# Hybrid RWKV7 and NSA forward pass on one core: scaled keys loaded two units ahead, small loads on GpSimd's queue, and the second pair's heads crossed

## The chip, the cores and the metric

The kernel runs on one core of a Trainium2 chip. The metric is the device time of the whole launch in microseconds (us); lower is better. A core has five instruction streams that run side by side and wait for each other through semaphores: PE (TensorE, matmuls; PEld is its loading of weights), DVE (VectorE), ACT (ScalarE), POOL (GpSimd) and SP (SyncE, which here only issues DMAs). A matmul in fp32 appears in the records as two instructions.

## The reference

Two layers over 256 tokens of width 2048. The first is an RWKV7 mixer of 32 heads of size 64, the second a sparse attention (NSA) that the change does not touch.

```python
def wkv7_scan(r, w, k, v, a, b):
    def step(S, inp):
        r_t, w_t, k_t, v_t, a_t, b_t = inp
        sa = jnp.einsum('bhvk,bhk->bhv', S, a_t)
        S = S * w_t[:, :, None, :] + sa[..., None] * b_t[:, :, None, :] + v_t[..., None] * k_t[:, :, None, :]
        return S, jnp.einsum('bhvk,bhk->bhv', S, r_t)
...
def rwkv7_mixer(u, ...):
    xx = token_shift(u) - u
    mixed = u[None] + xx[None] * mu[:, None, None, :]
    rkvz = jnp.einsum('nbtd,nde->nbte', mixed[:4], w_rkvz)
    ...                       # decay, a, kk from small projections; heads of 64
    o = wkv7_scan(rh, heads(decay), kh, vh, -kk, kk * ah)
    mean = jnp.mean(o, axis=-1, keepdims=True)
    var = jnp.mean(jnp.square(o - mean), axis=-1, keepdims=True)
    o = ((o - mean) * lax.rsqrt(var + GN_EPS)).reshape(B, T, D) * ln_g + ln_b
    bonus = jnp.sum(rh * kh * r_k, axis=-1, keepdims=True) * vh
    o = (o + bonus.reshape(B, T, D)) * jax.nn.silu(z)
    return o @ w_o, v
```

The second layer (`nsa_shared_kv`, `nsa_mixer`) reads the residual h + y, and a last `rmsnorm` gives the output.

## The kernel before

**Stages.** The launch has three stretches. Up to about 364 us it normalises the input, projects k, v and z, and turns decay, keys and the "a" vectors into *scaled keys*, which it keeps in DRAM (`spd`: for each of 16 head pairs 128 rows of 1284 numbers, 642 KB), with v and silu(z) beside them (`vd`, `zd`). From 364 to 764 us runs the recurrence. After it come the rest of the output projection, the shared keys and values and the second layer.

**The recurrence.** Each head's 256 tokens are cut into 4 chunks of 64, and inside a chunk the recurrence is written as products with 64x64 triangular matrices, whose 32x32 diagonal blocks are inverted beforehand (`stage_t`, on DVE). Two heads make a *pair* (128 partitions: head h lies on half h, `R[h]`), two pairs (x = 0, 1) make a *unit* U; there are 8 units. A unit runs 12 steps v: for chunk c = v // 3, phase p = v % 3 of `phase`:
- p = 0: the state's part of the sums, `ARS` times S (L999), then ACT copies X (L1001);
- p = 1: the inverse `Yb` times X (L1006), then ACT copies `uv` (L1008); at c = 0 also the bonus sums (L1014), the first rows by which a unit can be told in the trace;
- p = 2: the new state (L1019, DVE L1022 to L1024), the output (L1032) and the removal of the known part for the next chunk (L987).

The matmuls among these have 64 rows and 64 columns, a quarter of the 128x128 array: L999, L1006 and L1014 (and, in `prep`, G at L929 and Y at L939, and in `turn_y` L1080) take head h of either pair from half h and leave it on half h. Only the A steps' products at L962 run from each half to both.

**What lies between the steps.** After each step `fill(FILL[v])` puts so many steps of the dense r projection into PE's order: each is three matmuls of 256 columns (L586 to L588, a high and a low half of the weights and of the input). The 16 column blocks of r need 256 such steps, 48 of them ahead of unit 0, 32 in a unit. Two blocks share one PSUM bank (`rps`). When block 2U+2+x is done, `scale_r` (at v = 1 for x = 0 and v = 6 for x = 1 of unit U, for unit U+1) multiplies it with the scaled keys: DVE L916 reads the bank and `spl` and writes `spl`'s last part, DVE L917 makes `mb`, POOL L918 and L919 copy the decays and make `ARS`. The r step that follows writes the same bank again, so it waits for `mb`. `prep` turns unit U+1's scaled keys into its matrices at v = 3 to 10 (`AUX`), while `finish` (group norm, bonus, gate) and `turn_y` handle unit U-1; POOL's L1052 takes a power for the norm (`rg`). When r is complete, the fills take steps of the output projection instead (`o_part`, three pairs of matmuls of 512 columns, L568 to L571); this begins in unit 6.

**Loads.** `spl` has two buffers (units of even and odd number). Unit U+1's scaled keys are asked for at v = 0 of unit U (`load_spl`, L865), on SP, behind the eight small loads of `Yb` for unit U+1 (L880, put at v = 11 of the unit before), and the four of `uv` (L888), and between the weight loads `wraw` (L174). The small loads of `load_a` (L872, L873) and `load_y` (L880) move pieces of 16 KB. `stage_t(1)` inverts the blocks for units 4 to 7: POOL loads them (L755), DVE works on them during units 0 to 2 (L778 to L812), ACT transposes (L816), POOL stores them (L814, L818). `load_a(4)` needs them, and the line `sch.require(lambda: U // 4 in tdone)` puts whatever is left of them into the order at once, at v = 6 of unit 2.

**What sets the order.** From the start of the recurrence PE, DVE, ACT, POOL and SP each run their instructions in the order in which the code is written (`manual_schedule`). A clock in the code, `sch.t`, decides only where pieces of `stage_t(1)` and of the weight preparation (DVE's `wlo` L186, ACT's `whi` L200) are put between them.

Of the kernel before, what the change touches and what calls it, by code (L numbers as in the profile page):

```python
# [211 lines left out]
def hybrid_kernel(ctx: ExitStack, tc: tile.TileContext, a: dict, out: bass.AP):  # L212
# [413 lines left out]
    def phase_z(nb):  # L626
        ps = two()
        yield from rows_block(ps, "z", 512, last=nb == 3)
        for tt in range(2):
# [112 lines left out]
    def stage_t(b):  # L742
# [47 lines left out]
        for lv in (8, 16):  # L790
            for g in range(32 // (2 * lv)):
                o = 2 * lv * g
                hb = lv // 2
# [81 lines left out]
    def load_y(U):
        sch.require(lambda: U // 4 in tdone)
        for x in range(2):
            for h in range(2):
                for q in range(2):
                    nc.sync.dma_start(Yb[U % 2][64 * h + 32 * q:64 * h + 32 * q + 32, x, :, 32 * q:32 * q + 32],  # L880
                                      inverse(yvd[U // 4], ((2 * U + x) % 8) * 2 + h, q))
# [40 lines left out]
    def prep(step, U):  # L922
        if step == "G":
            GY[U] = accp("sa")
            gp = GY[U][:, 0:256].rearrange("p (x c t) -> p x c t", x=2, c=NCH)
            for x in range(2):
                for c in range(NCH):
                    for h in range(2):
                        PE.matmul(gp[R[h], x, c, :], A10[R[h], x, c, :], Yb[U % 2][R[h], x, c, 32:64], start=True, **mm)  # L929
# [3 lines left out]
            sch.t += 500  # L933
        elif step == "Y":
            yp = GY[U][:, 256:512].rearrange("p (x c t) -> p x c t", x=2, c=NCH)
            for x in range(2):
                for c in range(NCH):
                    for h in range(2):
                        PE.matmul(yp[R[h], x, c, :], T00[R[h], x, c, :], GS[U][R[h], x, c, :], start=True, **mm)  # L939
# [740 lines left out]
```

## Time and profile before

| quantity | value |
|---|---|
| time of three runs: median (lowest to highest) | 1327.75 us (1323.08 to 1332.2) |
| the profiled execution's own time | 1326.59 us |
| its span (first to last instruction) | 1324.8 us |
| granted TensorE clock, mean over the span | 0.94 |
| up to the recurrence | 0 to 363.8 us |
| recurrence | 363.8 to 764.0 us, PE busy 287.0 us, clock 0.82 |
| rest | 764.0 to 1324.8 us, PE busy 550.7 us, clock 1.00 |

The times of a unit are counted from one unit's first L1014 to the next one's. In a row of the timeline stand the start and the duration in us, the engine (SPq is SP's queue, where the time of a row is the issuing), the line, the operation, what it writes and reads, its shape and its count, and in brackets the idle time before it with the instruction that ended it. The rows of the stretches give the length, the busy time of PE, PEld, DVE, ACT and POOL with instruction counts, the granted clock, the busy share of the DMA engines and GB/s.

### The profile page before, as it was taken

To read this page: it belongs to the slowest core of one execution; us is meant where nothing else is said; L and a number is where in the kernel's file an instruction comes from. 1 tells how busy PE (TensorE), PEld (TensorE's weight loads), DVE (VectorE), ACT (ScalarE), POOL (GpSimd) and SP (SyncE) were. 2 spreads that over 40 slices of the span, in tenths; PEclk is the share of its full clock that TensorE was granted. 3 is DMA by queue.
4 is the path that set the end of the run, shared out by engine and by line. 5 is a ranking of instruction groups with operands and counts; after the bars stand their busy time and mean duration, and the time that the engine had idled before them with its cause. 6 is when DMAs were issued, how large, how long until landed. Compare 5 with 4: busy or idle time off the path is not lost.

```text
span 1324.8 us, 25503 instructions
## 1 busy us (share of the span) xinstructions
PE 1184.5 (89%) x9424; PEld 1029.0 (78%) x9424; DVE 867.9 (66%) x1896; ACT 713.5 (54%) x1673; POOL 270.3 (20%) x301
## 2 busy tenths in 40 slices
PE   7999999899938756568678899999999999999997
PEld 6788998878837656557666688888889999999887
DVE  6999776798934467234334568767547688776555
ACT  4667776666613323223334457666556666666553
POOL 2300154244330110111010000101023333333101
PEclk9999999998969787688679999999999999999999
DMA  6558877758776432544332467587665635463763
GB/s 218 166 182 247 223 237 235 198 178 237 218 157 147 125 105 68 170 113 104 94 113 93 148 209 245 176 265 222 207 172 151 160 99 141 120 158 114 272 205 112
DMA packets 243517, 225.26 MB, mean 170 GB/s; under 512 B 64016, under 2 KB 191424, under 8 KB 243008
## 3 DMA queue, kind: packets, MB, share of 16 engines
q1 hardware_dynamic: 242528, 220.98, 56.6%
q0 software_dynamic: 864, 2.65, 0.8%
q8 instruction: 74, 1.21, 0.4%
q14 instruction: 51, 0.42, 0.1%
HBM read 200.48 MB, written 23.10 MB: 169 GB/s over the span
## 4 chain that ended last, share of the span: by engine, by line
PE 76%; DVE 9%; DMA 6%; issue 3%; ACT 2%; SPq 2%; POOL 2%; DVEq 0%; ACTq 0%; POOLq 0%
PE bank L569 13%; PE bank L571 13%; PE bank L568 13%; PE bank L586 7%; PE bank L588 6%; PE bank L587 6%; PE bank L228 4%; DVE wlo L186 2%; DMA spl<-spd 2%; PE pair L999 1%; PE pair L1032 1%; SPq L888 1%; DMA wraw<-in_a_w_rkvz_dram 1%; DMA invA<-abd 1%; POOL sp L716 1%
## 5 line engine op out<-in xcount | busy, mean ns | idle before, releaser
L186 DVE TENSOR_TENSOR wlo<-wraw,whi 128x512 fp32r<-128x512 f32 (+2 forms) x612 | 437.3, 727 | 147.3 <-ACT whi L200 144.7
L200 ACT ACTIVATE whi<-wraw 128x512 fp32r<-128x512 f32 (+2 forms) x664 | 402.2, 619 | 219.4 <-PE bank L571 97.6
L586 PE MATMUL bank<-mh,whi 128*128 128x256 f32 (+1 forms) x800 | 247.3, 309 | 82.6 <-DVE mb L917 82.3
L569 PE MATMUL bank<-wlo,mh 128*128 128x512 f32 (+3 forms) x640 | 244.4, 383 | 4.0 <-DVE wlo L186 3.9
L571 PE MATMUL bank<-whi,ml 128*128 128x512 f32 (+3 forms) x640 | 242.0, 382 | 0.0
L588 PE MATMUL bank<-mh,wlo 128*128 128x256 f32 (+1 forms) x800 | 235.0, 294 | 0.8 <-DVE wlo L186 0.8
L587 PE MATMUL bank<-ml,whi 128*128 128x256 f32 (+1 forms) x800 | 235.0, 294 | 0.0
L586 PEld LDWEIGHTS bank<-mh,whi 128*128 128x128 f32 (+1 forms) x800 | 158.8, 199 | 92.1 <-DVE mb L917 64.0
L568 PE MATMUL bank<-whi,mh 128*128 128x512 f32 (+3 forms) x640 | 218.3, 382 | 4.0 <-ACT mh L412 2.4
L587 PEld LDWEIGHTS bank<-ml,whi 128*128 128x128 f32 (+1 forms) x800 | 159.6, 200 | 1.9
L588 PEld LDWEIGHTS bank<-mh,wlo 128*128 128x128 f32 (+1 forms) x800 | 159.0, 199 | 2.5 <-DVE wlo L186 1.0
L569 PEld LDWEIGHTS bank<-wlo,mh 128*128 128x128 f32 x640 | 121.2, 189 | 26.4 <-DVE wlo L186 7.5
L568 PEld LDWEIGHTS bank<-whi,mh 128*128 128x128 f32 x640 | 120.0, 189 | 23.9 <-ACT mh L412 2.6
L571 PEld LDWEIGHTS bank<-whi,ml 128*128 128x128 f32 x640 | 121.1, 189 | 19.6 <-issue 0.4
L186 POOL TENSOR_TENSOR wlo<-wraw,whi 128x512 fp32r<-128x512 f32 (+2 forms) x52 | 67.8, 1306 | 190.2 <-ACT whi L200 158.4
L569 PE MATMUL bank<-wlo,kvh 128*128 128x512 f32 x192 | 76.9, 401 | 0.0
L571 PE MATMUL bank<-whi,kvl 128*128 128x512 f32 x192 | 76.1, 396 | 0.0
L568 PE MATMUL bank<-whi,kvh 128*128 128x512 f32 x192 | 67.4, 396 | 0.0
L1073 ACT ACTIVATE O<-pair,nmr,rg 128x64 f32<-128x64 f32 x64 | 21.1, 401 | 66.2 <-DVE nmr L1059 66.2
L1042 DVE BATCH_NORM_STATS2 sta<-pair 128x6 f32<-128x64 f32 x64 | 13.8, 216 | 61.6 <-ACT X L1001 60.9
L1001 ACT ACTIVATE X<-pair 128x128 f32<-128x128 f32 x32 | 8.9, 277 | 81.3 <-PE pair L999 60.7
L412 ACT ACTIVATE mh<-mtmp 128x256 fp32r<-128x256 f32 x96 | 38.9, 410 | 22.3 <-DVE mtmp L419 20.7
(318 smaller groups left out, 1894.0 us busy)
## 6 DMA issues: line engine op xcount, KB each, us to landing
wraw<-in_a_w_rkvz_dram SPq DMA_DIRECT2D x128, 512.0 KB, 4.8
wraw<-in_kv_w_dram SPq DMA_DIRECT2D x48, 512.0 KB, 4.3
wraw<-in_b_w_in_dram SPq DMA_DIRECT2D x40, 512.0 KB, 4.3
wraw<-in_a_w_o_dram SPq DMA_DIRECT2D x32, 512.0 KB, 4.2
wraw<-in_b_w_o_dram SPq DMA_DIRECT2D x32, 512.0 KB, 3.6
spd<-sp SPq DMA_DIRECT2D x16, 642.0 KB, 5.0
spl<-spd SPq DMA_DIRECT2D x16, 642.0 KB, 5.3
wraw<-in_b_w_in_dram SPq DMA_DIRECT2D x24, 384.0 KB, 3.3
```

Of the source, the lines that this page charges most:

```text
L186: eng.tensor_tensor(lv, src, hv.bitcast(F32), op=OP.subtract)
L200: self.nc.scalar.activation(hv, src, AF.Copy)
L228: return fn(*args, **kw)
L412: S.activation(h, src, AF.Copy)
L568: PE.matmul(o, mh[:, ts], wh[:, 0, :], start=k == ends[0], stop=False)
L569: PE.matmul(o, mh[:, ts], wl[:, 0, :], start=False, stop=False)
L571: PE.matmul(o, ml[:, ts], wh[:, 0, :], start=False, stop=k == ends[1])
L586: PE.matmul(o, wh[:, s, :], mh, start=k == 0 and first, stop=False, **kw)
L587: PE.matmul(o, wh[:, s, :], ml, start=False, stop=False, **kw)
L588: PE.matmul(o, wl[:, s, :], mh, start=False, stop=k == NK - 1, **kw)
L1042: V.bn_stats(sta[:, x, c, :], view(U, 192 + 64 * c, 64)[:, x])
L1073: S.activation(O[:, x, i, :], view(U, 192 + 64 * i, 64)[:, x], AF.Identity, scale=rg[:, x, i:i + 1], bias=nmr[:, x, i:i + 1])
```

## The change

**Scaled keys.** At v = 0 of unit U the kernel now asks for unit U+2's scaled keys instead of unit U+1's, into the buffer that unit U has given up. The weights, scaled keys and v needed first are asked for ahead of the rest in the prologue, where `scale_r(0, 0)`, 8 r steps, the load of unit 1's scaled keys, 8 r steps and `scale_r(0, 1)` follow each other.

**Queues.** `load_a`, `load_y` and the last block of z are issued by GpSimd, the rest by SP as before. Around unit 4, SP's order before is the following; `spl_4673` and `spl_4674` are the scaled keys of unit 5's two pairs, which `scale_r` uses a step later in the same unit.

```order
L174 DMA wraw<-in_a_w_rkvz_dram 128x8x128
L880 DMA Yb_4670<-yvd_1623 32x4x32 x8
L888 DMA uv_4676<-vd 64x4x64 x4
L865 DMA spl_4673<-spd 128x1284
L865 DMA spl_4674<-spd 128x1284
L174 DMA wraw<-in_a_w_rkvz_dram 128x8x128 x2
```

Now, at the same place, the two buffers named 4670 and 4671 are those of unit 6.

```order
L176 DMA wraw<-in_a_w_rkvz_dram 128x8x128
L893 DMA uv_4675<-vd 64x4x64 x4
L868 DMA spl_4670<-spd 128x1284
L868 DMA spl_4671<-spd 128x1284
L176 DMA wraw<-in_a_w_rkvz_dram 128x8x128 x2
L903 DMA gb<-in_a_ln_g_dram 64x4x64
```

The loads of `Yb` have left SP's order there, and the scaled keys in it are used one unit later. On POOL, around v = 0 of a unit, stood:

```order
L1052 TENSOR_TENSOR rg<-rg,half 128x8
L885 MEMSET uv_4675 64x8x64 x2
L918 COPY pc<-spl_4671 128x4
L919 TENSOR_TENSOR ars_4681<-spl_4671 128x384
L918 COPY pc<-spl_4672 128x4
L919 TENSOR_TENSOR ars_4682<-spl_4672 128x384
L1052 TENSOR_TENSOR rg<-rg,half 128x8
```

Now the small loads of the next unit's blocks stand ahead of it (`a` and `t` are `A10` and `T00`):

```order
L875 DMA a_4666<-abd 32x4x32
L877 DMA t_4667<-tnd_1621 32x4x32
L885 DMA Yb_4668<-yvd_1623 32x4x32 x8
L1051 TENSOR_TENSOR rg<-rg,half 128x8
L890 MEMSET uv_4674 64x8x64 x2
L927 COPY pc<-spl_4670 128x4
L928 TENSOR_TENSOR ars_4680<-spl_4670 128x384
```

What moved: eight issues of `Yb` now come directly ahead of the power for the norm (`rg`, now L1051), which DVE's `nmr` waits for. `nmr` itself is now issued after `v` in step 1.

**Crossed heads.** For the second pair, `H(1, h)` is the other half: its operands `A10`, `T00`, `Yb`, X, O and the loads that fill them lie on half 1-h. So of the four 64x64 matmuls of a step, two run from a half to itself and two to the other half; the matmuls are written chunk by chunk with the pairs inside. G and Y now share a tile of two banks, and A0, A1 write that tile and one more bank, with DVE's three masks (M0, M1, M2) set apart; `turn_y` handles both pairs in one step.

**The inverses of the second half.** `stage_t(1)` starts 9000 ns later by the code's clock, and its costliest steps are counted at 1.8 instead of 2.4 times. On DVE, at v = 6 of unit 2, stood behind `scale_r`'s product:

```order
L917 TENSOR_TENSOR mb<-bank_4701,spl_4674 128x256
L811 TENSOR_TENSOR invX<-invT,invM 128x512
L812 TENSOR_REDUCE invT<-invX 128x8x8
L811 TENSOR_TENSOR invX<-invT,invM 128x1024
L812 TENSOR_REDUCE invT<-invX 128x8x8
L811 TENSOR_TENSOR invX<-invT,invM 128x1024
L812 TENSOR_REDUCE invT<-invX 128x8x8
L186 TENSOR_TENSOR wlo<-wraw,whi 128x512
```

and now stands:

```order
L926 TENSOR_TENSOR mb<-bank_4700,spl_4673 128x256
L803 TENSOR_TENSOR invX<-invA,invT 128x512
L804 TENSOR_REDUCE invM<-invX 128x8x8
L813 TENSOR_TENSOR invX<-invT,invM 128x512
L814 TENSOR_REDUCE invT<-invX 128x8x8
L813 TENSOR_TENSOR invX<-invT,invM 128x512
L814 TENSOR_REDUCE invT<-invX 128x8x8
L813 TENSOR_TENSOR invX<-invT,invM 128x1024
L814 TENSOR_REDUCE invT<-invX 128x8x8
L813 TENSOR_TENSOR invX<-invT,invM 128x1024
L814 TENSOR_REDUCE invT<-invX 128x8x8
L188 TENSOR_TENSOR wlo<-wraw,whi 128x512
```

The pieces of `stage_t(1)` that are put there at once have grown from three pairs of product and sum to five.

**The end.** In unit 6 all r steps are placed by v = 7 (`FILLL`) and none after; the output projection's steps start in unit 7, four r steps' worth at a time.

```diff
-AUX = {3: ("G",), 4: ("B0",), 5: ("Y",), 6: ("B1",), 7: ("A0",), 8: ("A1",), 9: ("A2", "T0"), 10: ("T1",)}
+AUX = {3: ("G",), 4: ("B0",), 5: ("Y",), 6: ("B1",), 7: ("A0",), 8: ("A1",), 9: ("M0", "M1"), 10: ("T", "M2")}
+AUXL = {3: ("G",), 4: ("B0",), 5: ("Y",), 6: ("B1",), 7: ("A0",), 9: ("A1",), 10: ("T", "M0", "M1"), 11: ("M2",)}
+FILLL = (2, 2, 2, 2, 2, 2, 2, 2, 0, 0, 0, 0)
...
-            store_heads(zd, nb, tt, th)
+            store_heads(zd, nb, tt, th, G if nb == 3 else nc.sync)
...
-        yield 500.0
+        yield 9000.0 if b else 500.0
...
-                        yield DT * (2.4 if b else 1.0)
+                        yield DT * (1.8 if b else 1.0)
...
-    psum = open_psum((("bank", 0), ("bank", 1), ("bank", 2), ("bank", 3), ("pair", 0), ("pair", 1)))
-    banks(acc=(0,), sa=(1, 2, 3))
+    psum = open_psum((("bank", 0), ("bank", 1), ("pair", 2), ("pair", 0), ("pair", 1)))
+    banks(acc=(0,), sa=(1,))
...
+    H = lambda x, h: R[h ^ x]
...
-                    nc.sync.dma_start(Yb[U % 2][64 * h + 32 * q:64 * h + 32 * q + 32, x, :, 32 * q:32 * q + 32],
-                                      inverse(yvd[U // 4], ((2 * U + x) % 8) * 2 + h, q))
+                    at = 64 * (h ^ x) + 32 * q
+                    G.dma_start(Yb[U % 2][at:at + 32, x, :, 32 * q:32 * q + 32],
+                                inverse(yvd[U // 4], ((2 * U + x) % 8) * 2 + h, q))
...
+            for c in range(NCH):
+                for x, h in each:
+                    PE.matmul(gp[R[h], x, c, :], A10[H(x, h), x, c, :], Yb[U % 2][H(x, h), x, c, 32:64], start=True, **mm)
...
-                        PE.matmul(o[R[h], x], ARS[U % 2][x][R[h], k, c - 1, :], st[R[h], x, :], start=False, **mm)
+                        PE.matmul(o[H(x, h), x], ARS[U % 2][x][R[h], k, c - 1, :], st[R[h], x, :], start=False, **mm)
...
-                PE.matmul(pu[R[h], x], Yb[U % 2][R[h], x, c, :], XS[U][R[h], x, :], start=False, **mm)
+                PE.matmul(pu[R[h], x], Yb[U % 2][H(x, h), x, c, :], XS[U][H(x, h), x, :], start=False, **mm)
...
+    W.late = True
+    load_spl(0)
     load_a(0)
-    load_spl(0)
     load_y(0)
+    fill(8)
     load_v(0)
-    W.late = True
-    fill(2)
+    load_y(1)
+    fill(8)
+    scale_r(0, 0)
     phase_done.add("scan")
-    load_y(1)
+    fill(8)
     load_spl(1)
-    load_v(1)
-    fill(14)
-    scale_r(0, 0)
-    fill(16)
+    fill(8)
     scale_r(0, 1)
...
-                    if U + 1 < NU:
-                        load_v(U + 1)
-                if 0 < U and U + 1 < NU:
-                    load_spl(U + 1)
+                if U + 1 < NU:
+                    load_v(U + 1)
+                if U + 2 < NU:
+                    load_spl(U + 2)
...
-            if v == 6 and U + 1 < NU:
+            if v == (6 if U + 2 < NU else 8) and U + 1 < NU:
                 scale_r(U + 1, 1)
...
-                for step in {1: ("nmr", "v", "02"), 2: ("25",), 3: ("58", "b"), 4: ("g",), 7: ("+",), 8: ("z",)}.get(v, ()):
+                for step in {1: ("v", "nmr", "02"), 2: ("25",), 3: ("58", "b"), 4: ("g",), 7: ("+",), 8: ("z",)}.get(v, ()):
...
-            fill(FILL[v] if "r" not in phase_done else FILLO)
+            fill(FILLO if U + 1 == NU else FILLL[v] if U + 2 == NU else FILL[v])
```

More of the change, by code (lines that the diff above doesn't have):

```diff
@@ L923, in prep @@
         if step == "G":
[L924 to L929, printed above, removed]
+            GY[U] = pair_tile(2).rearrange("p (x c) -> p x c", x=2)
+            gp = GY[U][:, :, 0:128].rearrange("p x (c t) -> p x c t", c=NCH)
+            for c in range(NCH):
+                for x, h in each:
+                    PE.matmul(gp[R[h], x, c, :], A10[H(x, h), x, c, :], Yb[U % 2][H(x, h), x, c, 32:64], start=True, **mm)
             gs = scan.tile([128, 2, NCH, 32], F32, name="gs", bufs=1)
@@ L932, in prep @@
             GS[U] = gs
-            sch.t += 500
+            sch.t += 550
         elif step == "Y":
[L935 to L939, printed above, removed]
+            yp = GY[U][:, :, 128:256].rearrange("p x (c t) -> p x c t", c=NCH)
+            for c in range(NCH):
+                for x, h in each:
+                    PE.matmul(yp[H(x, h), x, c, :], T00[R[h], x, c, :], GS[U][R[h], x, c, :], start=True, **mm)
             for h in range(2):
@@ L951, in prep @@
             sch.t += 300
+        elif step[0] == "A":
+            x = int(step[1])
+            if x == 0:
+                AT[U] = (pair_tile(2), accp("sa"))
+            both, m = AT[U]
+            BK, pp, kr, ar = parts(U, x)
+            for c in range(NCH):
+                o = x * 256 + c * 64
+                for e in range(2):
+                    for h in range(2):
+                        k = h ^ e
+                        PE.matmul(both[R[k], h * 512 + o:h * 512 + o + 64], BK[R[h], c, k, :], ar[R[h], 1, c, :], start=True, **mm)
+                for h in range(2):
+                    PE.matmul(m[R[1 - h], o:o + 64], BK[R[h], c, 1 - h, :], ar[R[h], 0, c, :], start=True, **mm)
+            sch.t += 900
@@ L1009, in phase @@
             if c == 0:
-                for x in range(2):
-                    for i in range(NCH):
-                        for h in range(2):
-                            o = x * 512 + 448 + 2 * i
-                            PE.matmul(PBK[U][R[h], o:o + 2], mb[R[h], x, 64 * i:64 * i + 64], ones2[R[h]], start=False, **mm)
+                for i in range(NCH):
+                    for x, h in each:
+                        o = x * 512 + 448 + 2 * i
+                        PE.matmul(PBK[U][H(x, h), o:o + 2], mb[R[h], x, 64 * i:64 * i + 64], ones2[R[h]], start=False, **mm)
             sch.t += 200
@@ L1188, in hybrid_kernel @@
     fill(LASTFILL - 2)
-    for x in range(2):
-        turn_y(U, x)
-        fill(3)
+    turn_y(U)
     for _ in dense:
```

102 lines of the change are left out of this document (43 added, 59 removed).

## The prediction

> **What bounds the kernel now.** The page's costliest groups came first. On one line PE stands idle for long behind DVE, which is not busy there.
>
> ```profile
> L586 PE MATMUL bank<-mh,whi 128*128 128x256 f32 (+1 forms) x800 | 247.3, 309 | 82.6 <-DVE mb L917 82.3
> ```
>
> Next the waits from 330 to 780 us (who <- releaser: sum, count, longest), to see what DVE itself waits for:
>
> ```profile
> PE bank L586 <- DVE mb L917: 82.3, 13, 20.2
> ...
> DVE spl L916 <- DMA spl<-spd: 63.7, 6, 14.7
> ```
>
> So an r step waits for `mb`, and DVE for the scaled keys. Where it lies in a unit the timeline of unit 4 shows:
>
> ```profile
> 582.94 2.32 SPq L880 DMA_DIRECT2D Yb<-yvd  x5
> 583.90 1.10 PE L1014 MATMUL pair<-ones,mb 64*64 64x2 f32 x32 [0.75 <-ACT uv L1008]
> 585.35 2.51 SPq L888 DMA_DIRECT2D uv<-vd  x4
> 587.95 1.02 SPq L865 DMA_DIRECT2D spl<-spd  x2
> 592.72 0.42 DVE L916 TENSOR_TENSOR spl<-bank,spl 128x256 f32<-128x256 f32 x1 [11.19 <-DMA spl<-spd]
> 593.53 0.58 PE L586 MATMUL bank<-mh,whi 128*128 128x256 f32 x1 [8.53 <-DVE mb L917]
> 613.33 0.39 PE L586 MATMUL bank<-mh,whi 128*128 128x256 f32 x1 [1.41 <-DVE mb L917]
> ```
>
> SP asks for the keys at 588, once the small loads are out; PE needs them at 585 and stands 8.53 us. The second `scale_r` costs 1.41: DVE's two products, whose data are there. Then the stretches, cut at the units' first L1014 (us, busy PE, PEld, DVE, ACT, POOL, clock, DMA share, GB/s); the last two rows split unit 4 after its stall:
>
> ```profile
> 394.40:408.60 14.20, 13.46 (x240) 12.38 (x239) 8.87 (x20) 5.76 (x14) 2.00 (x3) 1.00 0.81 188
> 408.60:440.40 31.80, 28.31 (x462) 24.87 (x462) 15.58 (x48) 11.11 (x30) 3.88 (x6) 0.95 0.55 137
> 440.40:482.40 42.00, 30.94 (x496) 27.36 (x496) 22.43 (x56) 14.04 (x40) 3.52 (x6) 0.84 0.33 95
> 482.40:536.80 54.40, 32.68 (x496) 28.79 (x496) 32.56 (x57) 16.27 (x44) 8.69 (x12) 0.75 0.39 120
> 536.80:583.90 47.10, 31.18 (x494) 27.59 (x494) 16.84 (x43) 14.13 (x40) 5.10 (x8) 0.78 0.42 120
> 583.90:628.90 45.00, 32.96 (x494) 29.22 (x494) 16.84 (x43) 14.13 (x40) 5.35 (x8) 0.77 0.44 113
> 628.90:673.30 44.40, 32.97 (x494) 29.22 (x494) 16.85 (x43) 14.12 (x40) 5.36 (x8) 0.77 0.35 102
> 673.30:719.60 46.30, 34.20 (x479) 27.75 (x479) 19.41 (x48) 15.18 (x42) 4.59 (x6) 0.82 0.34 105
> 719.60:764.00 44.40, 39.93 (x368) 29.94 (x369) 23.08 (x57) 21.06 (x54) 1.64 (x1) 1.00 0.42 131
> 586.10:606.40 20.30, 12.41 (x110) 11.26 (x111) 5.95 (x14) 5.67 (x17) 1.52 (x3) 0.50 0.38 112
> 606.60:630.30 23.70, 20.35 (x385) 17.76 (x383) 10.89 (x29) 8.25 (x23) 3.84 (x4) 1.00 0.49 114
> ```
>
> Unit 0 loads no keys, has no stall and takes 31.8 us; units 1 to 6 take 279.2 together. A stall is paid twice: PE idles, and the clock stands at 0.50 for the next 20 us.
>
> **Part 1: keys two units ahead.** They are now asked for a whole unit (some 30 us) before use; before, 4.8 us passed from request (587.95) to DVE's start (592.72). The first-`scale_r` stall goes from units 1 to 6, and with it the slow clock. What is late next is DVE's 1.41, twice a unit, as unit 0 shows it. A stall-free unit is therefore unit 0's 31.8, less 1.5 for its clock of 0.95, plus 1.2 for `turn_y`'s matmuls (two of the row below), which unit 0 lacks: 31.5. Unit 4 gives the same by another way: 45.0 − 8.5 − about 5 (half of what PE did in 20.3 us at half clock) = 31.5.
>
> **Part 2: crossed heads.** The timeline of unit 4 has both kinds of matmul, 64x64 in two quadrants and in four; the last row is from the chain of waits in the prologue:
>
> ```profile
> 608.80 1.12 PE L939 MATMUL bank<-gs,t 64*64 64x32 f32 x32
> 610.76 0.68 PE L999 MATMUL pair<-S,ars 64*64 64x64 f32 x16
> 618.23 0.69 PE L962 MATMUL bank<-spl 64*64 64x64 f32 x32
> 622.61 0.63 PE L1080 MATMUL pair<-cst,O 64*64 64x64 f32 x16
> ...
> 403.13 1.08 PE bank L975 x32
> ```
>
> 32 records take 0.69 in four quadrants (L962) and 1.08 to 1.12 in two (L939, L975): 0.41 less. A unit has 48 such records of L999 and 32 each of L1006, L1014, G, Y and `turn_y`, 208 in all: 208/32 × 0.41 = 2.7 us. The bounds: nothing, if some other limit holds these matmuls; 3.5 if all halve (7 us at 1.1 per 32). I take 2.7, since L962 runs the very pattern.
>
> **Part 3: issues on POOL.** Each steady unit gives POOL 16 issues. POOL's rows nearest to them are the loads of the inverses (median issue in ns in the middle), the power for the norm, and a store beside a DVE product:
>
> ```profile
> L755 POOL DMA_DIRECT2D invA<-abd x8: 628/628/732, 369.7 to 374.2; - x8
> ...
> 626.03 2.01 POOL L1052 TENSOR_TENSOR rg<-rg,half 128x8 f32<-128x8 f32 x1 [12.17 <-DVE rg L1051]
> ...
> 519.60 0.68 DVE L186 TENSOR_TENSOR wlo<-wraw,whi 128x512 fp32r<-128x512 f32 x1
> ...
> 519.98 0.65 POOL L814 DMA_DIRECT2D tnd<-invT  x1 [8.32 <-DVE invT L812]
> ```
>
> At 0.63 us, 16 issues are 10 us on top of POOL's 5.35 in unit 4, far below the unit's length. But the eight of `Yb` wait for the last reader of that buffer (L1006 at v = 10) and stand ahead of the power: 5 us, with some 3 us between that reader and the next unit's statistics, so `rg` comes about 2 us late. DVE's `nmr`, queued before `scale_r`'s next work, passes some of it on; the move of `v` ahead of `nmr` takes part of that away. I take +0.4 us a unit. SP loses 16 issues of 0.46 each (2.32 for five); its weights had the time before too: nothing. A steady unit: 31.5 − 2.7 + 0.4 = 29.2.
>
> **Part 4: unit 2.** Here DVE does the forced rest of the inverses:
>
> ```profile
> 503.31 1.09 DVE L801 TENSOR_TENSOR invX<-invA,invT 128x512 f32<-128x512 f32 x1
> ...
> 505.04 0.68 DVE L186 TENSOR_TENSOR wlo<-wraw,whi 128x512 fp32r<-128x512 f32 x1
> ...
> 510.98 1.58 DVE L811 TENSOR_TENSOR invX<-invT,invM 128x512 f32<-128x512 f32 x1
> ...
> 513.32 1.94 DVE L811 TENSOR_TENSOR invX<-invT,invM 128x1024 f32<-128x1024 f32 x1
> ...
> 522.45 0.69 PE L1019 MATMUL pair<-uv,bkt 128*64 128x64 f32 x8 [7.88 <-ACT uv L1008]
> ```
>
> Three product-and-sum pairs run from 510.98 to 519.60 (where `wlo` follows), and PE stands 7.88, since ACT's transposes of the result lie ahead of its `uv` copy. The order now has five pairs; the two new ones have 512 elements, at the 1.73 from 503.31 (a product; its sum follows) to 505.04: +3.5. So unit 2 is 29.2 + 11.4 for this stall + 3 for 3.2 us pairs (513.32 to 519.60 holds two) that stand ahead of the state's addition in the steps before + 6 for some 12 us of its rest at half clock: 49.6.
>
> The clock: unit 4's row has 0.50 for 20.3 us after a stall. The Trainium skill ("TensorE: Matmul & The Clock Gate", "Part 1: The HAM clock gate") has the full rate back after a busy window of about 3.4 us; by that the 6 would be an estimated 1.7 and the sum 1231. The trace does not agree, so the sum keeps 6.
>
> **Part 5: unit 6, the prologue and the end.** In unit 6 16 r steps go instead of 32; three matmuls of an r step take the 0.36 between the starts of their successors (613.79, then 614.15), so 29.2 − 5.8 + 1 for latency that fewer fills leave bare = 24.4. Unit 0: 31.8 − 2.3 (no `turn_y`) = 29.5.
>
> ```profile
> 613.79 0.28 PE L586 MATMUL bank<-mh,whi 128*128 128x256 f32 x1
> 614.15 0.28 PE L586 MATMUL bank<-mh,whi 128*128 128x256 f32 x1
> ...
> 382.98 0.18 DVE L761 COPY invT<-invA 128x16 f32<-128x16 f32 x1 [6.98 <-DMA invA<-abd]
> 386.03 0.55 PE L586 MATMUL bank<-mh,whi 128*128 128x256 f32 x1 [20.24 <-DVE mb L917]
> ...
> 758.70 0.39 PE L569 MATMUL bank<-wlo,mh 128*128 128x512 f32 x1
> ```
>
> The prologue's 20.24 ends at 386.03. DVE's copy for the inverses waits for POOL's loads until 382.98, and `scale_r` stands behind it; `stage_t(1)` now starts later, and the keys come first in SP's order. Then G is first to wait, for `A10` and `Yb`. On POOL, from the recurrence's start at 364: four stores of z at 0.63 (2.5), memsets (2, an estimate), 16 issues at 0.63 (10), and some 3 until the last has landed: 382. From G to the first L1014 the stretch from 394.4 took 14.2 us at full clock; less two crossed groups 13.4, plus 3.6 for a clock still low: 399, where before 408.6; I would not be surprised by 393 or 404.
>
> The output projection leaves unit 6, where the fills from v = 6 on held 5.1 of its steps (k), each six 512-column matmuls at 0.68 per three (from an L569 to the next, 758.70): 7.0 go to the end. Add 3 for unit 7, whose thinner fills may let the clock fall, less 1.2 for its crossed matmuls: +8.8.
>
> **Sum.** L1014 of unit 7 comes at 399 + 29.5 + 4 × 29.2 (units 1, 3, 4, 5) + 49.6 + 24.4 = 619.3, before 719.6: −100.3. With +8.8: −91.5. The profiled execution took 1326.6 (span 1324.8), 1.2 under the median of the three runs; 1326.6 − 91.5 = 1235.
>
> **Rivals.** *The crossing buys nothing.* L962's four quadrants write one PSUM bank for each row half, whereas every two-quadrant row above writes one bank from both halves, as the crossed matmuls of a pair still do; so the bank and not the quadrant may set the time. Then 2.7 × 7.5 = 20 us fall out: 1255. Chance 0.17. The Trainium skill ("TensorEngine Tiling (Array Packing)", "Gotcha 1: PSUM Pressure") states that different row tiles cannot use the same bank at once; by it this rival would hold. No row here separates the two.
>
> *POOL's issues cost 1.2 us* where other work runs: `rg` 4.6 us later in seven units, +32: 1267. For it: L755's longest is 0.73 in a quiet stretch; against: L814's 0.65 beside DVE's `wlo`. Chance 0.10.
>
> *More gain:* the prologue's G at 377, no clock fall in unit 7, the state's addition in unit 2 not held up, crossing at 3.5: −5 −3 −6 −6 = 1215. Chance 0.08.
>
> *POOL becomes the bound (slower).* Unit length is then 5.4 + 16 t for an issue time t. It decides from 29.2 = 5.4 + 16 t, t = 1.5; the kernel is slower than before from t = (44.4 − 5.4)/16 = 2.4. At 2.6 a unit takes 47, so 8 × 17.8 = +143: 1378. 0.65 beside a DVE product speaks against it. Chance 0.03. The Trainium skill ("SBUF — State Buffer", "A bandwidth-pool intuition that's wrong (but worth ruling out)") puts a GpSimd-issued DMA at 620 ns alone and 3100 ns beside a DVE copy, held back for its descriptors; an estimate by that is 5.4 + 16 × 3.1 = 55 a unit, some 1440. The trace agrees on the first figure and, in its one overlapped issue, not on the second.
>
> *The load ahead does not act*, because SP reaches it late behind its own waits for weight buffers: stalls stay, with the crossing and the queue as forecast: 1297. In unit 4 SP's rows follow each other without a wait from 582.94 to 588.97. Chance 0.02.
>
> **Numbers.** Forecast 1235 at 0.60. The range reaches down into the gain case and up to the POOL case: 1212 to 1268. The measurement tells about 1%, 13 us, from no change. Faster 0.93; slower 0.04 (POOL as bound, and a mishap of its size); within 1% 0.03.
>
> **What would show it.** Right: no L586 wait above 2 us on `mb` in units 1 to 6, units of about 29 at clock 1.00, 32 records of L939's successor at 0.7, POOL rows near 0.63, one long PE wait in unit 2 of 11 us. Wrong: POOL issues above 1 us with DVE's `nmr` waiting on `rg`; G, Y or L1006 at 1.1 per 32; or a stall on `spl<-spd` again.

## The result and the profile after

The changed kernel takes 1250.37 us (median of 4 runs, 1248.05 to 1252.28) against 1327.62 before: a ratio of 0.9417 (95% interval 0.9379 to 0.9456), 77 us less. The forecast was 1235 with a range of 1212 to 1268: right in sign and inside the range, 15 us too low. The profiled execution took 1252.2 (span 1250.4), 17.1 above the forecast's sum, and the stretches below show where these 17.1 lie.

From the page of the changed kernel, the engines and the group that stood 82.6 us before; from its waits, the same pair with its count and longest wait. Line numbers are the changed kernel's (L588 was L586, L926 was L917, L1013 was L1014).

```profile
PE 1162.2 (93%) x9424; PEld 1007.8 (81%) x9424; DVE 867.1 (69%) x1896; ACT 712.3 (57%) x1673; POOL 343.8 (27%) x433
...
L588 PE MATMUL bank<-mh,whi 128*128 128x256 f32 (+1 forms) x800 | 246.0, 307 | 14.5 <-DVE mb L926 14.3
...
PE bank L588 <- DVE mb L926: 14.3, 14, 2.1
```

The stalls of 6.6 to 12.0 us in units 1 to 6 have gone; what is left is DVE's own 1.4 once a unit, 0.5 once a unit and 2.1 in the prologue. No wait of DVE for the scaled keys is left among the larger ones.

The stretches from one unit's first L1013 to the next (units 0 to 6, then the rest; columns as before):

```profile
399.20:432.01 32.81, 28.57 (x463) 24.92 (x463) 17.27 (x59) 11.20 (x30) 11.20 (x20) 0.84 0.58 152
432.01:464.14 32.13, 27.80 (x495) 24.17 (x495) 21.20 (x61) 13.93 (x40) 13.88 (x24) 0.89 0.54 142
464.14:512.54 48.40, 30.74 (x495) 26.78 (x495) 36.55 (x62) 16.15 (x44) 17.20 (x26) 0.79 0.49 140
512.54:544.70 32.16, 27.83 (x495) 24.23 (x495) 16.16 (x43) 13.90 (x40) 14.30 (x24) 0.89 0.60 157
544.70:576.83 32.13, 27.80 (x494) 24.18 (x495) 16.13 (x43) 13.90 (x40) 14.14 (x24) 0.89 0.59 157
576.83:607.58 30.75, 26.42 (x491) 22.93 (x492) 16.05 (x43) 13.90 (x40) 13.76 (x24) 0.94 0.50 145
607.58:636.44 28.86, 22.57 (x449) 18.94 (x449) 15.27 (x42) 12.28 (x38) 5.58 (x8) 0.88 0.32 91
636.44:1250.40 613.96, 597.20 (x3572) 517.34 (x3572) 413.44 (x912) 363.82 (x837) 115.80 (x104) 0.99 0.57 174
```

| place | before | forecast | after | after − forecast |
|---|---|---|---|---|
| first bonus matmul of unit 0 | 408.6 | 399 | 399.2 | +0.2 |
| unit 0 | 31.8 | 29.5 | 32.8 | +3.3 |
| units 1, 3, 4, 5 | 41.9, 47.1, 45.0, 44.4 | 29.2 each | 32.1, 32.2, 32.1, 30.8 | +10.4 |
| unit 2 | 54.4 | 49.6 | 48.4 | −1.2 |
| unit 6 | 46.3 | 24.4 | 28.9 | +4.5 |
| from unit 7 to the end of the span | 605.2 | 614.0 | 614.0 | 0.0 |

So the prologue, unit 2 and the end came as forecast; units 0, 1 and 3 to 6 are longer by 1.6 to 4.5 us each, and in all of them the granted clock is 0.84 to 0.94, where the forecast had 1.00 (in unit 0 the 0.95 of before).

**Where the clock falls.** The timeline of the changed kernel around v = 1 of unit 4, PE beside ACT and DVE:

```profile
543.53 0.34 PE L1006 MATMUL pair<-X,Yb 64*64 64x64 f32 x8
544.08 0.57 ACT L1008 ACTIVATE uv<-pair 64x128 f32<-64x128 f32 x2 [0.74 <-PE pair L1006]
544.70 0.64 PE L1013 MATMUL pair<-ones,mb 64*64 64x2 f32 x32 [0.82 <-ACT uv L1008]
545.37 0.42 DVE L926 TENSOR_TENSOR mb<-bank,spl 128x256 f32<-128x256 f32 x1 [1.31 <-PE pair L1013]
545.85 0.42 PE L588 MATMUL bank<-mh,whi 128*128 128x256 f32 x1 [0.51 <-DVE mb L926]
```

From 543.87 to 545.85 PE does nothing but 0.64 us of matmuls of two columns: it waits for the copy of `uv` (its bank is read there), then DVE waits for the bonus matmuls (they read the `mb` that it is to overwrite), then PE for DVE. Cut at steps of 3.41 us, the stretches behind are:

```profile
542.69:546.10 3.41, 2.07 (x50) 1.72 (x49) 1.89 (x5) 1.19 (x5) 3.28 (x5) 1.00 0.86 210
546.10:549.52 3.42, 2.96 (x25) 2.55 (x26) 1.77 (x5) 1.69 (x5) 1.81 (x3) 0.50 0.90 250
549.52:552.93 3.41, 3.41 (x47) 3.07 (x44) 0.09 (x1) 1.51 (x5) 0.00 (x0) 0.50 0.93 323
559.76:563.17 3.41, 1.98 (x36) 1.61 (x37) 3.03 (x9) 1.28 (x3) 1.93 (x3) 1.00 0.55 115
```

The window with the hole is followed by two at clock 0.50; the full one among these is the last slow one. This hole became the first theory for the missing 17 us; the runs below test it.

### The profile page after: what moved, and what is told of

It is laid out like the page before. It is cut to its first block, busy times and chain, and to the rows that moved or that the text cites. A ratio compares the mean times of both kernels' runs of the same rounds, so it can differ in the third digit from the quotient of the medians.

```text
span 1250.4 us, 25597 instructions
## 1 busy us (share of the span) xinstructions
PE 1162.2 (93%) x9424; PEld 1007.8 (81%) x9424; DVE 867.1 (69%) x1896; ACT 712.3 (57%) x1673; POOL 343.8 (27%) x433
## 4 chain that ended last, share of the span: by engine, by line
PE 75%; DVE 11%; DMA 4%; issue 3%; ACT 3%; POOL 2%; SPq 1%; ACTq 0%; DVEq 0%; POOLq 0%
PE bank L571 12%; PE bank L573 12%; PE bank L570 12%; PE bank L588 8%; PE bank L589 6%; PE bank L590 6%; PE bank L230 4%; DVE wlo L188 3%; PE pair L573 1%; PE pair L570 1%; PE pair L1031 1%; PE pair L571 1%; ACT whi L202 1%; DMA Yb<-yvd 1%; DVE invX L803 1%
## 5 line engine op out<-in xcount | busy, mean ns | idle before, releaser
L588 PE MATMUL bank<-mh,whi 128*128 128x256 f32 (+1 forms) x800 | 246.0, 307 | 14.5 <-DVE mb L926 14.3
L571 PE MATMUL bank<-wlo,mh 128*128 128x512 f32 (+3 forms) x608 | 231.8, 382 | 5.2 <-DVE wlo L188 5.1
L573 PE MATMUL bank<-whi,ml 128*128 128x512 f32 (+3 forms) x608 | 228.4, 380 | 0.0
L570 PE MATMUL bank<-whi,mh 128*128 128x512 f32 (+3 forms) x608 | 204.7, 380 | 1.7 <-ACT mh L414 1.5
L588 PEld LDWEIGHTS bank<-mh,whi 128*128 128x128 f32 (+1 forms) x800 | 157.4, 197 | 24.1 <-DVE mb L926 14.2
L571 PEld LDWEIGHTS bank<-wlo,mh 128*128 128x128 f32 x608 | 115.3, 190 | 26.5 <-DVE wlo L188 8.7
L570 PEld LDWEIGHTS bank<-whi,mh 128*128 128x128 f32 x608 | 113.8, 189 | 20.3 <-ACT mh L414 1.7
L573 PEld LDWEIGHTS bank<-whi,ml 128*128 128x128 f32 x608 | 115.3, 190 | 17.7 <-issue 0.4
L421 DVE SCALAR_TENSOR_TENSOR mtmp<-xx,prm,xn 128x256 f32<-128x256 f32 x96 | 48.8, 517 | 0.6 <-POOL xx L506 0.5
```

The lines of the kernel that those rows point to most:

```text
L421: V.scalar_tensor_tensor(m, xx[:, k, :], mu[:, k:k + 1], xn[:, k, 1:], op0=OP.mult, op1=OP.add)
L570: PE.matmul(o, mh[:, ts], wh[:, 0, :], start=k == ends[0], stop=False)
L571: PE.matmul(o, mh[:, ts], wl[:, 0, :], start=False, stop=False)
L573: PE.matmul(o, ml[:, ts], wh[:, 0, :], start=False, stop=k == ends[1])
L588: PE.matmul(o, wh[:, s, :], mh, start=k == 0 and first, stop=False, **kw)
```

## The experiments

Every ratio is against the kernel before on the same chip, so kernels are compared by their ratios; the changed kernel stands at 0.9417.

### The bonus matmuls moved out of the hole

```diff
             if c == 0:
                 removal(U, 0)
+                for i in range(NCH):
+                    for x, h in each:
+                        o = x * 512 + 448 + 2 * i
+                        PE.matmul(PBK[U][H(x, h), o:o + 2], mb[R[h], x, 64 * i:64 * i + 64], ones2[R[h]], start=False, **mm)
...
-            if c == 0:
-                for i in range(NCH):
-                    for x, h in each:
-                        o = x * 512 + 448 + 2 * i
-                        PE.matmul(PBK[U][H(x, h), o:o + 2], mb[R[h], x, 64 * i:64 * i + 64], ones2[R[h]], start=False, **mm)
```

> The changed kernel, with the 16 bonus matmuls (L1013) issued at v = 0, right after the removal, instead of v = 1 between the uv copy and the r steps. Theory 'hole': the 17 us by which the recurrence is longer than forecast come from a hole of about 2 us at v = 1 of each unit (0.82 waiting for uv, 0.64 of two-column matmuls, 0.51 waiting for mb), after which the granted clock is 0.50 for some 7 us. Without the hole the clock of units 1, 3, 4 rises from 0.89 to 0.97 or more and a unit goes from 32.1 to 27.5 to 28.5: 25 to 30 us less, 1220 to 1226. Rival 'waits only': the clock falls for another reason; just the bare waits go, 1.3 us in 7 units: 1241, clock still 0.89.

Measured: 1239.70 us, ratio 0.9348 (0.9319 to 0.9377), some 10 us less. The total is what the rival named, but not by the rival's way. Units 3 to 6 and the 63 us after them (the marker now stands at v = 0, some 3 us earlier in each unit):

```profile
506.90:538.35 31.45, 27.03 (x498) 23.50 (x494) 16.67 (x45) 14.02 (x40) 14.57 (x26) 0.95 0.64 170
538.35:567.20 28.85, 25.29 (x498) 22.01 (x495) 16.07 (x45) 13.90 (x40) 13.47 (x24) 1.00 0.66 175
567.20:596.04 28.84, 25.27 (x498) 22.00 (x495) 16.06 (x45) 13.90 (x40) 13.44 (x24) 1.00 0.55 158
596.04:620.41 24.37, 18.85 (x451) 16.25 (x447) 14.79 (x44) 11.72 (x36) 6.09 (x9) 0.99 0.38 103
620.41:683.41 63.00, 57.93 (x442) 43.96 (x442) 32.91 (x75) 29.19 (x70) 4.42 (x4) 0.90 0.44 139
```

Units 4 and 5 take 28.85 us at clock 1.00, unit 6 24.4. Units 3 to 6 gain 10.4 us together, units 0 to 2 4.3. Some 4 are given back: at the start, where the first removal (L987) comes 2.1 later (397.37 against 395.29), and from unit 7 on, where the clock is 0.90 in the first 63 us instead of 0.97. With the hole gone the clock of units 4 and 5 is 1.00, as its theory said; the 25 to 30 us that it gave for the total were wrong, since the clock falls in other places too.

### The hole filled, with nothing moved

Three idle matmuls stand ahead of the bonus matmuls, two behind them, in units 0 to 6.

```diff
             if c == 0:
+                idle = pair_tile(2) if U + 1 < NU else None
+                for n in range(3 if U + 1 < NU else 0):
+                    PE.matmul(idle[:, 0:128], ident, ident, start=True, **mm)
                 for i in range(NCH):
...
+                for n in range(2 if U + 1 < NU else 0):
+                    PE.matmul(idle[:, 0:128], ident, ident, start=True, **mm)
```

> The changed kernel with five idle 128x128 matmuls (an identity by itself, into a PSUM tile that nobody reads) in units 0 to 6 at v = 1: three ahead of the bonus matmuls, two behind them. No wait of the program's own work is taken away; they only fill PE's hole, and can delay the r steps by some tenths. Theory 'hole': the clock no longer falls at v = 1, units 1, 3, 4 take 28.5 to 30 us instead of 32.1, about 10 us less as with the bonus matmuls moved, 1236 to 1245. Rival 'wait': the time went because the program's own waits went, not for the clock; then the fill gives nothing, or costs up to 4 us: 1250 to 1254.

Measured: 1239.55 us, ratio 0.9352 (0.9314 to 0.9390). The timeline at v = 1 of unit 3, and units 3 to 5:

```profile
504.38 0.34 PE L1006 MATMUL pair<-X,Yb 64*64 64x64 f32 x8
504.65 0.94 PE L1012 MATMUL pair<-cst 128*128 128x128 f32 x6
505.55 0.64 PE L1016 MATMUL pair<-ones,mb 64*64 64x2 f32 x32
506.12 0.71 PE L1018 MATMUL pair<-cst 128*128 128x128 f32 x4
506.71 0.39 PE L588 MATMUL bank<-mh,whi 128*128 128x256 f32 x1
...
505.55:535.31 29.76, 26.76 (x505) 23.33 (x505) 16.17 (x43) 13.93 (x40) 14.31 (x24) 1.00 0.57 154
535.31:566.47 31.16, 28.17 (x505) 24.66 (x505) 16.12 (x43) 13.94 (x40) 14.16 (x24) 0.95 0.62 161
566.47:595.85 29.38, 26.38 (x502) 22.97 (x501) 16.05 (x43) 13.93 (x40) 13.79 (x24) 1.00 0.53 151
```

Work that serves no result, put where PE stood idle, makes the kernel 9 to 11 us faster (by the ratios and by the medians; the two intervals overlap by 0.0011). Nothing of the program's own work became earlier (from the end of L1006 to the first L588 it is 1.99 us here and was 1.98); only the clock changed. That settles it against the rival: with clock 1.00 units 3 and 5 take 29.8 and 29.4 us, and 29.2 was the forecast. Unit 4 still falls to 0.95, behind its second `scale_r` (last section).

### The crossing undone, with and without the filled hole

In `load_a` and `load_y`, 64 * h stands for 64 * (h ^ x) as well. (`T00` lies on half h in either kernel; of the products that read it, Y, it is the output that crosses.)

```diff
-    H = lambda x, h: R[h ^ x]
+    H = lambda x, h: R[h]
```

> The changed kernel without the crossing: both pairs' heads lie on their own halves again, all else as changed. Theory 'quadrants' (the forecast's term of 2.7 us a unit): 32 records go from 0.64 to about 1.1, a unit grows by 2.7, the whole by about 20 us: 1270. Rival 'bank': the crossing bought nothing in time: 1250 within 5.

Measured: 1278.21 us, ratio 0.9644 (0.9601 to 0.9688), about 30 us longer than the changed kernel. More than the 20 expected; unit 6 and the end came 4.5 and 7 us longer, and the clock swings from unit to unit, as units 3 and 4 show, which run the same instructions:

```profile
519.44:551.53 32.09, 27.98 (x495) 24.63 (x495) 16.91 (x43) 13.79 (x40) 14.86 (x25) 1.00 0.57 146
551.53:587.77 36.24, 32.13 (x494) 28.44 (x494) 16.92 (x43) 13.93 (x40) 14.13 (x25) 0.86 0.54 139
```

So the same edit was held against the kernel with the filled hole:

> The changed kernel without the crossing and with the five idle matmuls at v = 1, to be held against the crossed kernel with the same idle matmuls (units of 29.2 to 31.2 us at a clock near 1.00, 1239.6 us in all). Theory 'quadrants': at equal clock a unit is 2.7 longer, 32 us; the whole 18 to 24 us longer: 1258 to 1264; the other 8 us of the 28 that the straight kernel lost were the clock. Rival: the crossing is worth 3.5 to 4 us a unit by itself: 1268 to 1272.

Measured: 1262.10 us, ratio 0.9528 (0.9500 to 0.9555), 0.0176 above the crossed one: 23 us. Units 3 to 5:

```profile
513.97:546.12 32.15, 29.19 (x506) 25.86 (x505) 16.25 (x43) 13.93 (x40) 15.17 (x25) 1.00 0.54 142
546.12:578.24 32.12, 29.17 (x506) 25.84 (x505) 16.87 (x43) 13.82 (x40) 14.12 (x24) 1.00 0.64 157
578.24:610.03 31.79, 28.83 (x503) 25.50 (x502) 16.89 (x43) 13.82 (x40) 13.80 (x23) 1.00 0.51 142
```

At equal clock the crossing is worth 2.4 us a unit (32.15 against 29.76, 31.79 against 29.38), near the forecast (2.7). What the rest of the 30 was is not told apart: the profiled executions differ by 23 us without the filled hole (spans of 1273.7 and 1250.4) and by 20 with it (1258.7 and 1238.7), and without it the clock differs in both directions (units 0, 3 and 5 at 1.00 in the straight kernel, units 1 and 4 at 0.86, unit 6 at 0.80).

### The small loads back on SP

The same is done for `T00` and `Yb`.

```diff
-                G.dma_start(A10[at:at + 32, x, :, 0:32],
+                nc.sync.dma_start(A10[at:at + 32, x, :, 0:32],
```

> The changed kernel with A10, T00 and Yb loaded on SP's queue again, all else as changed. Forecast's theory: POOL's queue costs 0.4 us a unit through the power for the norm, so 3 us less inside the units; the prologue's G, which now waits for POOL's 16 issues until 382, comes up to 5 us earlier: 1242 to 1250. Rival 'POOL queue': the missing 17 us are those of the issues on POOL (rg, nmr late): 1230 to 1235.

Measured: 1244.27 us, ratio 0.9384 (0.9362 to 0.9406): 4 us less, with an interval that overlaps the changed kernel's. The units hardly change (31.6, 47.2, 31.8, 32.1 for units 1 to 4; 2.4 us less in units 0 to 6 together); where the clock is the same there is no difference (unit 4: 32.1 in both at 0.89, unit 6: 28.8 and 28.9 at 0.88). The first bonus matmul comes at 395.0 instead of 399.2. So POOL's queue costs the prologue about 4 us, and in the units no cost is seen. On POOL in the changed kernel, the loads' issue (median in the middle, ns) and the power for the norm ahead of unit 4:

```profile
L885 POOL DMA_DIRECT2D Yb<-yvd x64: 548/548/551, 371.0 to 605.9; - x64
...
539.90 3.25 POOL L885 DMA_DIRECT2D Yb<-yvd  x6
543.17 1.79 POOL L1051 TENSOR_TENSOR rg<-rg,half 128x8 f32<-128x8 f32 x1
```

The power starts 0.35 after DVE's last statistics (542.82) and ends at 544.96, before DVE, which is held by the bonus matmuls until 545.37, could take it.

### The keys late again in the changed kernel, and early in the kernel before

```diff
-                if U + 2 < NU:
-                    load_spl(U + 2)
+                if 0 < U and U + 1 < NU:
+                    load_spl(U + 1)
```

> The changed kernel with each unit's scaled keys asked for at v = 0 of the unit before, as in the kernel before, all else as changed. Theory: the mb stalls of units 1 to 6 return, 5 to 9 us each (SP's queue is shorter by eight issues of 0.46) and 5 us of slow clock each in place of today's 3: 6 x (7 + 2) = +54, 1295 to 1320. Rival 'the queue did it': with the small loads off SP the keys arrive in time anyway: under 1265.

Measured: 1289.53 us, ratio 0.9725 (0.9699 to 0.9752): 41 us longer. The timeline around v = 1 of unit 4:

```profile
565.44 1.02 SPq L868 DMA_DIRECT2D spl<-spd  x2
569.83 0.42 DVE L925 TENSOR_TENSOR spl<-bank,spl 128x256 f32<-128x256 f32 x1 [7.83 <-DMA spl<-spd]
570.64 0.58 PE L588 MATMUL bank<-mh,whi 128*128 128x256 f32 x1 [6.73 <-DVE mb L926]
```

The stall returns, 5.6 to 7.4 us in each of units 1 to 6, although SP has no `Yb` load ahead of the keys any more. The total is 5 us below the range: the six stalls make 37 of the 41 us, so the slow clock added less than 1 us a unit where 2 were expected; the units had one anyway.

The other way round, the one edit in the kernel before:

> The kernel before with one edit: at v = 0 of unit U it asks for unit U+2's scaled keys instead of unit U+1's. Theory: the mb stalls of units 1 to 6 (53.5 us together) go and with them 2 to 5 us of slow clock each; unit 2 keeps its 7.9 for the inverses; prologue and end stay as they are: 62 to 83 us less, 1243 to 1265. Rival 'needs the queue too': with the small loads still on SP ahead of them the keys or the weights behind them come late and half of the stalls stay: 1290 or more.

Measured: 1268.69 us, ratio 0.9568 (0.9548 to 0.9587): 57 us less, 4 short of the expected range. No stall on the keys is left, but an ordinary unit takes 34.3 at clock 0.90, not the 31.5 at 1.00 that the forecast's first part had:

```profile
521.35:555.65 34.30, 30.33 (x494) 26.73 (x494) 16.48 (x43) 14.05 (x40) 5.53 (x8) 0.90 0.58 159
```

This single edit makes three quarters of the whole gain.

### The inverses of the second half spread out

```diff
-                        yield DT * (1.8 if b else 1.0)
+                        yield DT * ((0.8 if lv == 8 else 2.2) if b else 1.0)
...
-                yield DT * (0.6 if b else 0.25)
+                yield DT * (0.3 if b else 0.25)
```

> The changed kernel with the pieces of the second half's inverses spread otherwise (factors 0.3 for the small levels, 0.8 for the middle and 2.2 for the last level), so that none is left to be put at once at v = 6 of unit 2; the same work in all. Theory: unit 2's 48.4 is its 11.06 wait for the inverses, the DVE products ahead of the state's addition and the slow clock behind; the wait goes, the products stay: unit 2 at 35 to 39, the others as they were, 9 to 13 us less: 1237 to 1242. Rival 'DVE is full there': the same 20 us of products delay the state's additions by as much: 1246 to 1252.

Measured: 1245.23 us, ratio 0.9382 (0.9357 to 0.9406), between the two cases and with an interval that overlaps the changed kernel's. In the changed kernel PE waits 11.06 in unit 2 (first row); with the pieces spread, units 1 and 2 are:

```profile
498.57 0.69 PE L1018 MATMUL pair<-uv,bkt 128*64 128x64 f32 x8 [11.06 <-ACT uv L1008]
```

```profile
432.96:469.77 36.81, 29.08 (x495) 25.35 (x495) 29.49 (x63) 13.92 (x40) 13.96 (x24) 0.86 0.48 134
469.77:507.75 37.98, 31.66 (x494) 27.52 (x494) 24.01 (x50) 16.11 (x44) 16.45 (x26) 0.78 0.62 178
```

Unit 2 gains 10.4, unit 1 loses 4.7, where DVE's busy time rises from 21.2 to 29.5: nearly half of the gain is lost again, since the products now stand in DVE's order there.

### Joined kernels

The first joins the bonus matmuls at v = 0, all small loads on SP and the spread inverses.

> The changed kernel with bonus matmuls at v = 0, small loads on SP and the inverses spread, as in the three runs that did one of these each. If the effects add: 1250 - 10 - 5 - 11 = 1224 (1218 to 1232). If the slow clock only moves on to another place: 1232 to 1240.

Measured: 1233.54 us, ratio 0.9309 (0.9275 to 0.9342): the effects do not add. The profiled execution, the longest of the four (a span of 1239.6), shows a new wait in unit 3: G waits for `Yb`. The run with only the small loads on SP has no such wait above 0.4 us in its units; why it comes here stays open.

```profile
505.62 0.99 PE L937 MATMUL pair<-Yb,a 64*64 64x32 f32 x6 [3.25 <-DMA Yb<-yvd]
```

The second therefore leaves the small loads on POOL, but for unit 0's (A10, T00 and Yb), puts the bonus matmuls at v = 0 and two idle matmuls at v = 1, and lets the inverses start earlier in the prologue (the flag "scan" starts `stage_t(1)`); the lines of the bonus and idle matmuls are like those above and are left out here:

```diff
-                G.dma_start(A10[at:at + 32, x, :, 0:32],
+                (G if U else nc.sync).dma_start(A10[at:at + 32, x, :, 0:32],
...
     load_y(0)
+    phase_done.add("scan")
...
-    phase_done.add("scan")
...
-                        yield DT * (1.8 if b else 1.0)
+                        yield DT * ((0.6 if lv == 8 else 2.0) if b else 1.0)
...
-                yield DT * (0.6 if b else 0.25)
+                yield DT * (0.25 if b else 0.25)
```

> The changed kernel with bonus matmuls at v = 0, two idle matmuls at v = 1 of units 0 to 6, the small loads of unit 0 alone on SP (the rest stays on POOL), and the second half's inverses started in the prologue and spread (factors 0.25, 0.6, 2.0), none left for one burst. Theory: no hole, no late Yb (which the run with all small loads on SP had in its fourth unit), unit 2 without its 11 us: units of 29 at clock 1.00, unit 2 at 34 to 38, first L1013 at 393 to 396: 1215 to 1226. Rival 'DVE is full': the spread inverses delay units 0 to 2 by what the burst cost: 1228 to 1236.

Measured: 1220.76 us, ratio 0.9215 (0.9184 to 0.9245): 2.1% below the changed kernel (0.9215/0.9417), the fastest of all. Units 1, 2 and 4:

```profile
423.88:460.49 36.61, 30.28 (x501) 26.30 (x499) 32.11 (x61) 15.06 (x42) 13.84 (x23) 0.81 0.49 137
460.49:491.30 30.81, 26.24 (x503) 22.56 (x499) 17.32 (x48) 14.91 (x42) 15.94 (x27) 0.99 0.81 223
522.49:551.33 28.84, 25.84 (x502) 22.52 (x498) 16.05 (x45) 13.93 (x40) 13.45 (x24) 1.00 0.65 175
```

The inverses are done by unit 2, and unit 1 pays for them (DVE 32.1 of 36.6 us). The third starts them 3000 ns earlier by the code's clock.

> As the joined kernel of this call, with the inverses started 3000 ns earlier by the code's clock, so that more of them lies in the prologue, where DVE is busy 11 of 36 us. Theory: unit 1 and 2 shorter by 2 to 4 us, unless DVE's copy for the inverses, which waits for POOL's loads, holds the weights' low halves back: 1212 to 1224; in that case the first L1013 comes 3 to 6 us later and the time is 1222 to 1232.

Measured: 1228.83 us, ratio 0.9282 (0.9249 to 0.9315). Units 2 to 5 all take 28.6 to 28.9 at clock 1.00, but the first bonus matmul comes 5.2 us later than in the second (397.8 against 392.6) and unit 0 takes 2.2 longer (33.5 against 31.3): the second of the two cases named. In the prologue PE waits 7 us for a low half of the weights, which the second does not do:

```profile
379.64 0.58 PE L590 MATMUL bank<-mh,wlo 128*128 128x256 f32 x1 [6.98 <-DVE wlo L188]
```

## Why the prediction was right, and where it was off

**Keys two units ahead: right.** The stalls went from units 1 to 6, nothing took their place, and undoing the one edit brings them back (41 us), making it alone brings 57 us.

**The stall-free unit: this step failed.** "Unit 0's 31.8, less 1.5 for its clock of 0.95" took the slow clock of unit 0 for something that a stall-free unit would not have, and struck it out. It comes behind the hole at v = 1 (the slow stretch of the kernel before starts at 411.9, its first L1014 at 408.6), which in the later units lay next to the long stall: with the keys early and nothing else changed they stand at 0.90. In the changed kernel the bonus matmuls in the hole are shorter (0.64, not 1.10) and a wait of 0.51 for `mb` has come behind them. Units 1 and 3 to 5 kept 3.4 to 6.8 us at half clock, unit 0 some 10, which begin at 395.9 already, behind the waits of the prologue. Measured with the hole filled, units 3 and 5 take 29.8 and 29.4. Half of the slow stretches, an estimate of their cost, is 12 us in units 1, 3, 4 and 5, where the table has +10.4, and in unit 0 3.4 more than before, where it has +3.3. Two readings of the step were off besides: unit 0 shows DVE's 1.41 once (at 425.68), not twice; and half of the 12.41 us in unit 4's row is 6.2, not 5, so that the second way gives 30.3. That way had struck out the slow clock as well, so it was no independent check.

**Crossed heads: right in kind and nearly in size.** 2.7 us a unit forecast, 2.4 at equal clock; 32 records of the bonus matmuls went from 1.10 to 0.64. The rival "buys nothing" is out. The Trainium skill's rule ("TensorEngine Tiling (Array Packing)", "Gotcha 1: PSUM Pressure"), by which that rival would have held, cost no time that these runs show, though both row halves of a pair still write one bank.

**POOL: 0.4 us a unit forecast, none measured;** an issue takes 0.55, not 0.63. The rivals with 1.2 us and more did not occur in any of 64 `Yb` issues (0.548 to 0.551); those from 539.90 ran beside DVE's `wlo`. The 3100 ns that the Trainium skill ("SBUF — State Buffer", "A bandwidth-pool intuition that's wrong (but worth ruling out)") has beside a DVE copy was not seen in an issue beside these products. What the queue costs lies in the prologue, 4 us, and there the forecast had counted it (399 against 399.2): PE's last wait for `Yb` ends at 381.08, forecast 382. That the rest fits as well is in part luck, since PE then waits 1.82 for POOL's memset of `uv` (until 395.29), which the sum did not have.

**Unit 2: right** (49.6 against 48.4): its stall came at 11.06 against the forecast 11.4; the other terms were not told apart. When the inverses were spread, unit 1 lost 4.7 of the 10.4 us that unit 2 gained.

**Unit 6: 24.4 forecast, 28.9 measured.** Its two slow stretches of 3.4 us (610.9 and 631.4) cost an estimated 3.4 of the 4.5. With the hole filled it still takes 27.6 at clock 0.94. (The 24.4 of the run with the bonus matmuls moved is no match: counted from v = 0, it lacks unit 7's v = 0.) The forecast had +1 for latency that fewer fills leave bare; after the last fill PE stands 3 us, while DVE works through the masks and the statistics:

```profile
631.22 0.74 PE L987 MATMUL pair<-uv,ama 128*64 128x64 f32 x8 [3.02 <-DVE sta L1041]
```

**The end: right** as a sum (+8.8 forecast and measured); its terms were not told apart, so it may be luck.

**On the clock rule,** the forecast said that the trace does not agree with a return after 3.4 us of work. That reading was half right. Of unit 4's 20.3 slow us, 6.8 had PE idle and 6.8 had it busy 2.75 and 2.95 of 3.41; but one window busy throughout did not bring the full rate back either (last section).

## What to carry to other kernels

When a stall is removed, do not strike out the slow clock beside it: look for what else in the same stretch leaves PE idle or doing tiny matmuls, since that can hold the clock down once the stall is gone. Here a dependent chain of 2 us (matmul, copy, two-column matmul, elementwise product, matmul) was followed by 3.4 to 6.8 us at half clock; five idle matmuls inside it paid. And work that is spread over an engine which runs in order still stands ahead of something there: unit 1 lost nearly half of what unit 2 gained.

## What the runs showed of the hardware that was not expected

The granted clock changes on a fixed grid. Taken from the clock in pieces of half a microsecond, the slow stretches between 360 and 690 us (start, length in us) are:

```
before:      371.0 20.5, 411.9 3.4, 442.7 13.7, 483.6 17.1, 517.8 10.2, 538.2 20.5, 586.0 20.5, 630.4 20.5, 674.8 17.1
after:       365.2 3.4, 375.4 10.2, 395.9 13.6, 433.4 6.8, 467.6 3.4, 477.8 3.4, 491.5 13.6, 515.4 6.8, 546.1 6.8,
             580.2 3.4, 610.9 3.4, 631.4 3.4, 669.0 3.4
hole filled: 365.6 3.4, 375.9 10.2, 471.4 10.2, 485.1 13.7, 549.9 3.4, 618.2 3.4, 655.8 6.8
```

Every length is one to six times 3.41 us, and within a run the starts lie whole multiples of 3.41 apart (in the changed kernel 395.9 to 433.4 is 11 of them). The Trainium skill ("TensorE: Matmul & The Clock Gate", "Part 1: The HAM clock gate") names windows of about 3.4 us for both directions and calls them free-running; the trace agrees with the length and with the grid.

What a window must hold to bring the half clock, or to end it, is not settled. In the four window rows of the changed kernel above, one with PE busy 2.96 of 3.42 is followed by another slow one and one with 3.41 ends it; and one with 2.07 busy, at v = 1, lowers the clock, while one with 1.98, at v = 6, does not. Three more rows, of the kernel before, the changed kernel and the one with the filled hole, show that busy time alone does not decide:

```profile
599.69:603.10 3.41, 3.41 (x52) 3.12 (x52) 1.32 (x6) 1.26 (x5) 0.00 (x0) 0.50 0.02 5
```

```profile
668.95:672.37 3.42, 2.84 (x7) 2.29 (x8) 2.94 (x5) 0.25 (x1) 0.00 (x0) 0.50 0.47 129
```

```profile
546.53:549.94 3.41, 1.98 (x27) 1.53 (x28) 1.64 (x7) 2.04 (x5) 0.54 (x1) 1.00 0.79 167
```

The first is busy throughout, mostly with 64x64 matmuls, and is followed by another slow one; the second, 2.84 busy with 128x128 matmuls of 512 columns, ends the half clock; the third, 1.98 busy at v = 6, lowers the clock (it makes unit 4 of that kernel 31.2 us long). How matmuls of different shapes are counted was not tried by itself. What the rows do show is that PE need not be idle for the clock to fall, and that the 20 us in the kernel before are windows of idling followed by windows that were not enough to end it. Since the grid does not move with the program, where a hole falls in it changes from unit to unit, which fits that units with the same instructions took 32.1 and 36.2 us (the straight kernel above), and that gains here do not add.
